# Where the gated activations of five down projections start in SBUF, relative to their weights, modulo 256 bytes

## The chip, the cores and the metric

The kernel runs on one core of a Trainium2 chip. The metric is device time in microseconds from launch to end. A core has TensorE (PE in the profile; PEld is its weight load, a row of its own that runs beside the matmuls), VectorE (DVE), ScalarE (ACT), GpSimd (POOL) and the DMA queues, here mostly that of SyncE (SP). Operands lie in SBUF, 128 partitions with the same byte address in each; TensorE reads both operands of a matmul from there and writes to PSUM. Below, the *distance* of a matmul is the address of its stationary operand minus the address of its moving operand, modulo 256 bytes.

## The reference, cut to what matters

A stack of two blocks works on 256 tokens of width 1024, all float32. It holds five feed-forward layers of this form (4 in the first block, 1 in the second, which has 16 more tokens in its mixer and the same 256 in its feed-forward layer), with a gated delta-rule mixer, a windowed attention and a retention and latent attention mixer between them:

```python
def swiglu(h, w_gu, w_down):
    gate, up = jnp.split(h @ w_gu, 2, axis=-1)
    return (jax.nn.silu(gate) * up) @ w_down

x = x + 0.5 * swiglu(rmsnorm(x, ffn1_norm[layer]), ffn1_w_gu[layer], ffn1_w_down[layer])
```

The inner width is 2816, so a down projection is a product of 256 x 2816 by 2816 x 1024.

## The kernel before, in words

Activations lie transposed, width on the partitions: `X[d]` is a 128 x 256 tile of the residual stream. A float32 product is made of three matmuls in the type `fp32r`: each operand is split into a high part and the remainder, and `lin` (lines 365 to 375) adds high x high, high x low and low x high for every 128-row piece of the contraction. The weight is the stationary operand (128 columns), the activation the moving one (256 columns). `Stream` loads weights in chunks of 128 x 2048 from SP's queue and splits each piece of 512 columns into `whi` (ScalarE, line 355) and `wlo` (VectorE, line 356), eight buffers each, from which TensorE takes slices of 128 columns.

`ffn` (line 459 on) runs five times, named "10", "20", "11", "21" and "30" in the order of the program. It first makes 44 gate and up projections of 24 matmuls each from `xh` and `xl`, the split and normed input. For each of 22 pairs it forms `ffg` and `ffu`, multiplies them, and splits the result into `ah` and `al`. The down projection then makes 8 output tiles, each of 22 x 3 = 66 matmuls with `ah` or `al` moving and `whi` or `wlo` stationary, and adds each to `X[d]`. `after(d)` prepares the next stage's input. Nothing is scheduled elsewhere: the order on each engine is that of the code.

Addresses follow from the order in which pools are opened. A `Home` has a pool `lines`, for tiles of whole multiples of 512 bytes, and a pool `rest`. Fill tiles that nothing reads or writes (`fill_cp`, `fill_sp`, `fill_wp`) move what is opened after them; the last is 512 - `LEAD` bytes long, and `LEAD` is 64. In the built program every `whi` and `wlo` slice starts at 32 modulo 256, and every `xh`, `xl`, `ah`, `al`, `dec`, `oh`, `ol` that `lin` moves past them starts at 224. The distance is thus 64 in the products that `lin` makes with 128 weight columns. A product with fewer columns goes through distances: in that of the delta rule's gates (`Stream("aba")`, 16 weight columns) one slice starts 64 bytes after the other, and the distance is 64, 128, 192 and 0 in turn, changing with every triple. The few other `fp32r` products lie outside `lin` or turn the roles round: the retention's scores (lines 1108 to 1110, distance 0, 64 contraction rows, 256 columns) and two small projections of the latent attention (line 1272 is one: the weight moves with 384 columns and the activation is stationary; distance 192).

Of the kernel before, what the change touches and what calls it, by code (L numbers as in the profile page):

```python
# [9 lines left out]
F32 = mybir.dt.float32  # L10
# [7 lines left out]
P = 128  # L18
# [13 lines left out]
LEAD = 64  # L32
CP_FILL = 320
SP_FILL = 448

# [184 lines left out]
def kernel(ctx: ExitStack, tc: tile.TileContext, dram: dict, out: bass.AP, dump=None):  # L222
# [8 lines left out]
    @contextmanager  # L231
    def home(name):
        with tc.tile_pool(name=name, bufs=1) as lines, tc.tile_pool(name=name + "r", bufs=1) as rest:
            yield Home(lines, rest)

    def pool(name, bufs=1, **kw):
        return ctx.enter_context(tc.tile_pool(name=name, bufs=bufs, **kw))
# [4 lines left out]
    rest = pool("sp", 2)  # L242
    rest.tile([P, SP_FILL // 4], F32, tag="fill", name="fill_sp", bufs=1)
    sp = Home(None, rest)
# [7 lines left out]
    def nm(base):  # L252
        uid[0] += 1
        return f"{base}_{uid[0]}"

    def sb(at, shape, tag, dt=F32, bufs=None):

        kw = {} if bufs is None else {"bufs": bufs}
        free = int(np.prod(shape[1:]))
        whole = -(-free * 4 // LINE) * LINE // 4  # L260
        if not isinstance(at, Home):
            return at.tile(shape, dt, tag=tag, name=nm(tag), **kw)
        if at.lines is None or whole != free and (dt != F32R or free * 4 < LINE):
            return at.rest.tile(shape, dt, tag=tag, name=nm(tag), **kw)
        if whole == free:
            return at.lines.tile(shape, dt, tag=tag, name=nm(tag), **kw)
        assert len(shape) == 2
        return at.lines.tile([shape[0], whole], dt, tag=tag, name=nm(tag), **kw)[:, :free]

    def bank(pool, shape):  # L270
        return pool.tile(shape, F32, tag="bank", name=nm("bank"))
# [95 lines left out]
    def lin(o, st, off, xs, w=P, n=S, ks=None):  # L367

        last = len(xs) - 1
        for k in range(len(xs)) if ks is None else ks:  # L370
            xh, xl = xs[k]
            wh, wl = st.at(off + k * w, w)
            mm(o, wh, xh[:, :n], start=k == 0, stop=False)  # L373
            mm(o, wl, xh[:, :n], start=False, stop=False)  # L374
            mm(o, wh, xl[:, :n], start=False, stop=k == last)  # L375

    def split(src, hi, lo):
        A.copy(hi, src)  # L378
        V.tensor_tensor(lo, src, f32(hi), op=ALU.subtract)  # L379
# [60 lines left out]
    def opening(norm, jobs, stats=None, n=S, at=(5, 1)):  # L440


        a, b, c = ((lambda ks, j=j: lin(*j[0], ks=ks, **j[1])) for j in jobs)
        stats = stats or (lambda: rnorm_nat(norm.ssq, D))
        a(range(KD - 1))
        b(range(at[0]))
        if at[0] < KD - 1:
            rn = stats()
        b(range(at[0], KD - 1))
        a([KD - 1])  # L450
        b([KD - 1])
        if at[0] >= KD - 1:
            rn = stats()
        c(range(at[1]))
        r = row_bcast(rn, n)
        c(range(at[1], KD))
        return r

    def ffn(name, norm, after, scale, hook=None, gu=None, first=None):

        with home(nm("ffn")) as fp:
            gu = gu or Stream("gu" + name)
            acts = []
            def proj(i):
                return bank(ps, [P, S]), gu, i * D, norm.xs

            pre = {i: proj(i) for i in range(3)}
            if first:
                first()
            r = opening(norm, [(pre[i], {}) for i in range(3)], at=(KD - 1, 3) if first else (5, 1))  # L470
            for m in range(KF):
                for i in (2 * m, 2 * m + 1):
                    if i not in pre:
                        pre[i] = proj(i)
                        lin(*pre[i])
                pg, pu = pre.pop(2 * m)[0], pre.pop(2 * m + 1)[0]
                g = sb(fp, [P, S], "ffg", bufs=2)
                V.tensor_tensor(g, pg, r[:, :S], op=ALU.mult)  # L478
                u = sb(fp, [P, S], "ffu", bufs=2)
                V.tensor_tensor(u, pu, r[:, :S], op=ALU.mult)  # L480
                A.activation(g, g, AF.Silu)  # L481
                V.tensor_tensor(u, g, u, op=ALU.mult)  # L482
                ah = sb(fp, [P, S], f"ah{m}", F32R)
                al = sb(fp, [P, S], f"al{m}", F32R)
                split(u, ah, al)
                acts.append((ah, al))
            dn = Stream("dn" + name)
            for d in range(KD):
                pd = bank(ps, [P, S])
                lin(pd, dn, d * FF, acts)  # L490
                if hook:
                    hook(d, pd)
                V.scalar_tensor_tensor(X[d][:, :S], pd, scale, X[d][:, :S], op0=ALU.mult, op1=ALU.add)
                after(d)
# [929 lines left out]
    def squares():  # L1424
# [6 lines left out]
        load_rest()  # L1431

    ffn("10", n, feed("mix_norm0"), 0.5, None, gu, squares)
    if dump:
        dump("x1", X[0][:, :S])
    n = cur[0]
    deltanet(n, feed("ffn2_norm0"))
    if dump:
        dump("x2", X[0][:, :S])
    n = cur[0]  # L1440
    ffn("20", n, feed("ffn1_norm1"), 0.5)
    n = cur[0]
    ffn("11", n, feed("mix_norm1"), 0.5)
    n = cur[0]
    window(n, feed("ffn2_norm1"))
# [94 lines left out]
```

## Time and profile before

| | us |
|---|---|
| median of 3 runs | 1472.96 (1472.29 to 1474.13) |
| the profiled execution, its own time | 1473.83 |
| its span, first to last instruction | 1472.0 |
| PE busy in it | 1443.5 (98%) |
| PEld busy | 1405.1 (95%) |
| DVE / ACT / POOL busy | 1107.7 / 858.2 / 114.1 |

[...] What a run of matmuls costs is the difference of the starts, called the *cadence* below: three rows of `lin` make a triple. A share of busy time near 100% says that the engine had work, not that it streamed a column in every cycle. [...]

### The profile page before, as it was taken

How to read it: one execution, taken by the hardware profiler on the slowest of the kernel's cores; microseconds unless marked ns; L12 is line 12 of the kernel's file. 1: busy time of each engine (PE TensorE's matmuls, PEld its weight loads, DVE VectorE, ACT ScalarE, POOL GpSimd, SP SyncE). 2: the span in 40 equal slices, each digit the busy share in tenths (PEclk: the TensorE clock that was granted, in tenths of full speed). 3: DMA queues.
4: the chain of work that ended last, by engine and by line, in shares of the span. 5: the costliest groups of instructions: out<-in, count | busy, mean ns of one | idle time of the engine just before them, and what ended most of it. 6: DMA issues, size and time to landing. Idle time of an engine off the chain costs nothing.

```text
span 1472.0 us, 31018 instructions
## 1 busy us (share of the span) xinstructions
PE 1443.5 (98%) x12318; PEld 1405.1 (95%) x12318; DVE 1107.7 (75%) x2340; ACT 858.2 (58%) x1767; POOL 114.1 (8%) x123
## 2 busy tenths in 40 slices
PE   8999999998999999999999999999999999999997
PEld 8999999988999999999997999999999889999997
DVE  6877668886877767777678877788877758777764
ACT  6655567655655555555547655665545756665552
POOL 2000141101100010000100100012001000100000
PEclk9999999999999999999999999999999999999998
DMA  7655443551555555555550555555432425555551
GB/s 254 224 195 201 171 148 116 166 167 33 181 191 198 201 189 185 201 195 187 193 199 30 201 178 195 177 196 172 134 113 91 144 87 195 207 199 187 193 197 58
DMA packets 46368, 248.34 MB, mean 169 GB/s; under 512 B 11408, under 2 KB 16272, under 8 KB 17168
## 3 DMA queue, kind: packets, MB, share of 16 engines
q1 hardware_dynamic: 45680, 245.87, 49.0%
q8 instruction: 97, 1.59, 0.4%
q10 hardware_dynamic: 544, 0.50, 0.1%
q14 instruction: 47, 0.39, 0.1%
HBM read 243.99 MB, written 2.36 MB: 167 GB/s over the span
## 4 chain that ended last, share of the span: by engine, by line
PE 86%; DVE 7%; ACT 2%; DMA 2%; issue 1%; POOL 1%; DVEq 0%; POOLq 0%; ACTq 0%; SPq 0%
PE bank L375 26%; PE bank L373 26%; PE bank L374 26%; DVE wlo L356 2%; PE bank L1130 1%; PE bank L1350 1%; DVE cv L652 1%; ACT whi L355 1%; PE bank L979 1%; DMA tc<-s 1%; PE bank L1319 1%; DVE xl L395 0%; DMA s<-tb 0%; PE bank L969 0%; POOL rr L383 0%
## 5 line engine op out<-in xcount | busy, mean ns | idle before, releaser
L356 DVE TENSOR_TENSOR wlo<-raw,whi 128x512 fp32r<-128x512 f32 x922 | 641.2, 700 | 257.4 <-ACT whi L355 255.9
L355 ACT CAST whi<-raw 128x512 fp32r<-128x512 f32 x922 | 565.4, 618 | 444.8 <-PE bank L375 407.3
L373 PE MATMUL bank<-xh,whi 128*128 128x256 f32 (+1 forms) x2488 | 697.0, 280 | 1.3 <-DVE xt L513 1.0
L374 PE MATMUL bank<-xh,wlo 128*128 128x256 f32 (+1 forms) x2488 | 692.9, 279 | 2.1 <-DVE wlo L356 2.1
L375 PE MATMUL bank<-xl,whi 128*128 128x256 f32 (+1 forms) x2488 | 692.3, 278 | 1.1 <-DVE xl L395 1.0
L374 PEld LDWEIGHTS bank<-xh,wlo 128*128 128x128 f32 x2488 | 468.5, 188 | 3.6 <-DVE wlo L356 3.1
L373 PEld LDWEIGHTS bank<-xh,whi 128*128 128x128 f32 x2488 | 466.9, 188 | 4.2 <-issue 2.1
L375 PEld LDWEIGHTS bank<-xl,whi 128*128 128x128 f32 x2488 | 466.9, 188 | 2.2 <-DVE xl L395 1.7
L375 PE MATMUL bank<-al,whi 128*128 128x256 f32 x880 | 243.8, 277 | 0.0
L373 PE MATMUL bank<-ah,whi 128*128 128x256 f32 x880 | 243.8, 277 | 0.0
L374 PE MATMUL bank<-ah,wlo 128*128 128x256 f32 x880 | 243.8, 277 | 0.0
L374 PEld LDWEIGHTS bank<-ah,wlo 128*128 128x128 f32 x880 | 165.9, 189 | 0.0
L375 PEld LDWEIGHTS bank<-al,whi 128*128 128x128 f32 x880 | 165.2, 188 | 0.0
L373 PEld LDWEIGHTS bank<-ah,whi 128*128 128x128 f32 x880 | 165.2, 188 | 0.0
L407 POOL TENSOR_TENSOR ssq<-sq,ssq 128x256 f32<-128x256 f32 (+1 forms) x72 | 63.8, 886 | 1080.4 <-ACT sq L406 1070.8
L378 ACT CAST ah<-ffu 128x256 fp32r<-128x256 f32 x110 | 44.7, 407 | 26.2 <-DVE ffu L482 26.1
L482 DVE TENSOR_TENSOR ffu<-ffg,ffu 128x256 f32<-128x256 f32 x110 | 46.7, 425 | 4.6 <-ACT ffg L481 1.2
L478 DVE TENSOR_TENSOR ffg<-bank,r 128x256 f32<-128x256 f32 x110 | 46.6, 424 | 2.8 <-PE bank L375 2.2
L481 ACT ACTIVATE ffg<-ffg 128x256 f32<-128x256 f32 x110 | 45.3, 414 | 5.7 <-DVE ffg L478 5.4
L480 DVE TENSOR_TENSOR ffu<-bank,r 128x256 f32<-128x256 f32 x110 | 46.6, 423 | 0.3
L379 DVE TENSOR_TENSOR al<-ffu,ah 128x256 fp32r<-128x256 f32 x110 | 46.0, 418 | 0.5 <-ACT ah L378 0.5
L373 PE MATMUL bank<-dec,whi 128*128 128x256 f32 x128 | 36.7, 286 | 0.0
(360 smaller groups left out, 1426.4 us busy)
## 6 DMA issues: line engine op xcount, KB each, us to landing
raw<-gu SPq DMA_DIRECT2D x109, 1024.0 KB, 4.8
raw<-dn SPq DMA_DIRECT2D x55, 1024.0 KB, 4.9
raw<-wret SPq DMA_DIRECT2D x12, 1024.0 KB, 4.9
raw<-aqk SPq DMA_DIRECT2D x8, 1024.0 KB, 4.8
raw<-wga SPq DMA_DIRECT2D x8, 1024.0 KB, 4.8
raw<-bin SPq DMA_DIRECT2D x6, 1024.0 KB, 4.9
raw<-az SPq DMA_DIRECT2D x4, 1024.0 KB, 4.8
raw<-av SPq DMA_DIRECT2D x4, 1024.0 KB, 4.9
```

The source lines that it names most:

```text
L355: A.copy(hi[:, :n], raw[:, o : o + n])
L356: V.tensor_tensor(lo[:, :n], raw[:, o : o + n], f32(hi[:, :n]), op=ALU.subtract)
L373: mm(o, wh, xh[:, :n], start=k == 0, stop=False)
L374: mm(o, wl, xh[:, :n], start=False, stop=False)
L375: mm(o, wh, xl[:, :n], start=False, stop=k == last)
L378: A.copy(hi, src)
L379: V.tensor_tensor(lo, src, f32(hi), op=ALU.subtract)
L407: G.tensor_tensor(acc[:, :n], q[:, :n], acc[:, :n], op=ALU.add)
L478: V.tensor_tensor(g, pg, r[:, :S], op=ALU.mult)
L480: V.tensor_tensor(u, pu, r[:, :S], op=ALU.mult)
L481: A.activation(g, g, AF.Silu)
L482: V.tensor_tensor(u, g, u, op=ALU.mult)
```

## The change

Each `ffn` opens its pool `lines` with a fill tile whose length depends on the layer. Nothing reads or writes it. It moves `ah`, `al`, `ffg` and `ffu` of that layer up by so many bytes; their pool is closed at the end of the layer, so no other tile moves.

```diff
+PLACE = {"10": 128, "20": 32, "11": 224, "21": 160, "30": 96}
...
     def ffn(name, norm, after, scale, hook=None, gu=None, first=None):

         with home(nm("ffn")) as fp:
+            if PLACE[name]:
+                fp.lines.tile([P, PLACE[name] // 4], F32, tag="fill", name=nm("fill_fp"))
             gu = gu or Stream("gu" + name)
             acts = []
```

In the built program the activations of the five down projections start at 96, 0, 192, 128 and 64 modulo 256, in the order "10", "20", "11", "21", "30", where all started at 224; the weights stay at 32. The distances are 192, 32, 96, 160 and 224. Every engine has the same instructions in the same order with the same waits.

## Rows read from the trace of the kernel before

**Rows 1.** The page: busy time by engine; the chain that ended last, by engine and line.

```profile
PE 1443.5 (98%) x12318; PEld 1405.1 (95%) x12318; DVE 1107.7 (75%) x2340; ACT 858.2 (58%) x1767; POOL 114.1 (8%) x123
...
PE 86%; DVE 7%; ACT 2%; DMA 2%; issue 1%; POOL 1%; DVEq 0%; POOLq 0%; ACTq 0%; SPq 0%
PE bank L375 26%; PE bank L373 26%; PE bank L374 26%; DVE wlo L356 2%; PE bank L1130 1%; PE bank L1350 1%; DVE cv L652 1%; ACT whi L355 1%; PE bank L979 1%; DMA tc<-s 1%; PE bank L1319 1%; DVE xl L395 0%; DMA s<-tb 0%; PE bank L969 0%; POOL rr L383 0%
```

**Rows 2.** The page's costliest groups: matmuls of the down projections; last number: idle before.

```profile
L373 PE MATMUL bank<-ah,whi 128*128 128x256 f32 x880 | 243.8, 277 | 0.0
```

**Rows 3.** Tile `ah` in each down projection: ns min/median/max, first and last start.

```profile
L373 PE MATMUL bank<-ah,whi x176: 276/276/276, 135.2 to 194.7; 128*128 128x256 f32 x176
...
L373 PE MATMUL bank<-ah,whi x176: 276/276/276, 503.9 to 563.4; 128*128 128x256 f32 x176
...
L373 PE MATMUL bank<-ah,whi x176: 276/276/276, 684.4 to 743.9; 128*128 128x256 f32 x176
...
L373 PE MATMUL bank<-ah,whi x176: 281/281/281, 953.0 to 1014.9; 128*128 128x256 f32 x176
...
L373 PE MATMUL bank<-ah,whi x176: 276/276/276, 1400.8 to 1460.3; 128*128 128x256 f32 x176
```

**Rows 4.** Windows of "10" down, "11" gate/up, "21" gate/up, "21" down; columns first.

```profile
core 0: us, PE busy (x) PEld busy (x) DVE busy (x) ACT busy (x) POOL busy (x), PEclk, DMA share, GB/s
...
135.00:195.00 60.00, 60.00 (x532) 60.00 (x531) 37.67 (x62) 32.43 (x59) 5.23 (x6) 1.00 0.54 188
...
570.00:684.00 114.00, 114.00 (x1008) 114.00 (x1007) 89.06 (x171) 67.81 (x128) 0.00 (x0) 1.00 0.57 192
...
834.00:952.00 118.00, 118.00 (x1005) 118.00 (x1004) 90.31 (x172) 68.98 (x132) 0.00 (x0) 1.00 0.55 187
952.00:1015.00 63.00, 63.00 (x538) 63.00 (x537) 53.24 (x99) 42.45 (x81) 12.44 (x12) 1.00 0.54 183
```

**Rows 5.** Timeline of PE after a pause, in "21" and "30": start, duration.

```profile
834.22 0.60 PE L435 MATMUL bank<-tabs,rn 128*128 128x128 f32 x4
834.58 0.36 PE L373 MATMUL bank<-xh,whi 128*128 128x256 f32 x1
834.78 0.28 PE L374 MATMUL bank<-xh,wlo 128*128 128x256 f32 x1
834.90 0.28 PE L375 MATMUL bank<-xl,whi 128*128 128x256 f32 x1
835.02 0.28 PE L373 MATMUL bank<-xh,whi 128*128 128x256 f32 x1
...
1286.96 0.29 PE L374 MATMUL bank<-xh,wlo 128*128 128x256 f32 x1
1287.08 0.28 PE L375 MATMUL bank<-xl,whi 128*128 128x256 f32 x1
1287.20 0.28 PE L373 MATMUL bank<-xh,whi 128*128 128x256 f32 x1
...
1287.43 0.28 PE L375 MATMUL bank<-xl,whi 128*128 128x256 f32 x1
1287.54 0.28 PE L373 MATMUL bank<-xh,whi 128*128 128x256 f32 x1
```

**Rows 6.** Timeline of PE: the delta rule's gates, 16 weight columns, four distances in turn.

```profile
195.07 0.28 PE L373 MATMUL bank<-xh,whi 128*16 128x256 f32 x1
...
195.41 0.28 PE L373 MATMUL bank<-xh,whi 128*16 128x256 f32 x1
...
195.75 0.28 PE L373 MATMUL bank<-xh,whi 128*16 128x256 f32 x1
...
196.09 0.28 PE L373 MATMUL bank<-xh,whi 128*16 128x256 f32 x1
...
197.11 0.28 PE L373 MATMUL bank<-xh,whi 128*16 128x256 f32 x1
```

**Rows 7.** Timeline of PE: the retention's scores, distance 0.

```profile
1038.54 0.28 PE L1108 MATMUL bank<-rk1h,rk0h 64*128 64x256 f32 x1
1038.66 0.28 PE L1109 MATMUL bank<-rk1l,rk0h 64*128 64x256 f32 x1
1038.78 0.28 PE L1110 MATMUL bank<-rk1h,rk0l 64*128 64x256 f32 x1
```

**Rows 8.** Timeline of PE: a latent projection with moving weights, 384 columns, distance 192.

```profile
1147.08 0.34 PE L1273 MATMUL bank<-whi,cl 128*128 128x384 f32 x1
1147.25 0.34 PE L1274 MATMUL bank<-wlo,ch 128*128 128x384 f32 x1
...
1148.12 0.34 PE L1273 MATMUL bank<-whi,cl 128*128 128x384 f32 x1
```

## The prediction, written before the result was known

> **What bounds the kernel now.** The page comes first: TensorE has work for 98% of the span and holds 86% of the chain that ended last, nearly all of it on the three lines of `lin` [rows 1]. So only the time of a matmul, or a pause between matmuls, counts. The down projections, 2640 matmuls in three groups of 880, had no idle time before them [rows 2]; the windows of one show VectorE busy for 37.67 of 60 us, ScalarE for 32.43, and DMA at 0.54 [rows 4]. None of these is near becoming the bound, so whatever a matmul of a down projection gains or loses goes straight to the end of the kernel.
>
> Next the cadence. In tile `ah`, first and last start are 175 triples apart. In "10" that is 194.7 - 135.2 = 59.5 us, 0.340 us a triple, 0.1133 us a matmul; "20", "11" and "30" agree to the tenth of a microsecond. In "21" it is 1014.9 - 953.0 = 61.9 us, 0.1179 us a matmul [rows 3]. The gate and up projections ahead show the same pair: about 1008 matmuls take 114 us in "11" and 1005 take 118 us in "21" [rows 4]. [...] So the kernel has **two cadences for one and the same distance**, a fast one of 0.1133 us and a slow one of 0.1179 us, and a stretch keeps the one it falls into. After a pause both first show 0.12 us; in "21" it stays near that, in "30" it drops to 0.11 after four or five matmuls [rows 5]. [...]
>
> **The change part by part.** No instruction is added, removed or moved, and no wait changes; the fill tile costs no instruction. `ffg`, `ffu`, `ah` and `al` move by 32 to 224 bytes. Should VectorE or ScalarE write them more slowly, the slack just named hides it (VectorE 89.06 and ScalarE 67.81 of 114 us during gate and up projections, rows 4); cost nothing, and if this cover went, the last `ah` of a layer would arrive late, five times. What is left is the cadence in 5 x 528 matmuls. One nanosecond in all of them is 2.64 us.
>
> What a new distance does to the cadence no row shows for this shape, so I bound it.
>
> From above: the retention's scores at distance 0 start 0.12 us apart [rows 7]. [...] For the four fast layers 4 x 528 x 0.0067 = 14.1 us, for "21" 528 x 0.0021 = 1.1 us: **+15 us**.
>
> From below: four matmuls of 128 columns with full weight loads take 0.60 us against 0.28 us for one, so (0.60 - 0.28)/3 = 0.107 us apart [rows 5]. [...] Allowing 0.110 us, half way to the fast cadence, the gain would be 4 x 528 x 0.0033 = 7.0 us and 528 x 0.0079 = 4.2 us in "21": **-11 us**.
>
> Between them: with 16 weight columns the distance passes through 64, 128, 192 and 0, and the starts stay 0.34 us apart per triple, first to last (197.11 - 195.07)/6 [rows 6]. That says that the distance at the start of a load does not set the cadence; but the load is an eighth as long there, so it does not say that a full load keeps out of the moving operand's way. I take the two cadences of rows 3 as the only ones held over hundreds of matmuls of this shape; the 0.12 us of rows 7 is three matmuls long and looks like the start-up of rows 5. A layer whose distance changes has to find its cadence anew at its first down matmul, and nothing in the rows favours the fast one. So of the four fast layers I let two fall to the slow cadence, each 528 x 0.0046 = 2.4 us, together 4.9 us, and leave "21" where it is. From the profiled execution's 1473.83 us (a span of 1472.0 and 1.8 around it) that makes 1478.7 us; from the median, 0.9 us lower, 1477.8 us. I name **1478 us**.
>
> The work between the layers keeps its addresses, and its cadence is settled after a pause [rows 5], so I charge nothing there. If a later stretch did fall to the other cadence, its price would be some 1000 x 0.0046 = 4.6 us, either way.
>
> The row says that cadence differs while both operands stay where they are. [...]
>
> **The rivals.**
>
> *The distance has no part in it.* For it: rows 6, and the two cadences at one distance [rows 3]. [...] All five layers keep their cadence, "21" perhaps falling into the fast one for 2.4 us less: 1471 to 1474 us, call it 1473 us.
>
> [...]
>
> [...]
>
> *Every other distance is worse.* The weight load, 128 columns long, meets the moving operand in the same part of SBUF, and distance 64 is the one that avoids it: the bound from above, 0.12 us everywhere, +15 us: 1488 us.
>
> *The change does nothing.* A fill that is never used might have been dropped; the built program has the new addresses, so this is out.
>
> **How the numbers follow.** Forecast (one to four layers fall to the slow cadence, +2 to +10 us) 0.34; no part 0.27; faster start 0.21; all worse 0.18. The range from 1463 to 1490 us takes in all four centres with a few microseconds on the outside of the last two; by itself the forecast has 1475 to 1483 us. A difference of 0.2%, 2.9 us, is about the least that a measurement of this kernel can tell from none. Slower: 0.18 and most of 0.34 (all but one layer's worth), 0.47. Same: 0.27 and the rest, less a little for a faster "21", 0.31. Faster: 0.22.
>
> **What would show it.** First and last start of `ah` in each layer give five cadences. Forecast: each is 0.113 or 0.118 us, with at least one change among the four. No part: 0.1133 four times. [...] All worse: 0.12 and above. Gate and up projections should keep 114 us, 118 us in "21"; if they change, the step that the work between keeps its cadence is wrong. A distance with a cadence far beyond 0.12 us, or pauses inside a down projection, would upset the bounds.

## The result: 1.0% slower, and where it was lost

The changed kernel took 1488.57 us (median of 4, 1482.55 to 1490.64) against 1472.62 us; the ratio is 1.0102, 95% interval 1.007 to 1.0134. Timed once more in a later session it was 1.0086, 1.0053 to 1.012 (e11 below). The range of the prediction, 1463 to 1490 us, holds it, and the likelier sign was right; but the forecast of 1478 us had a third of the loss, and the time lies outside the forecast's own 1475 to 1483 us.

The profiled execution took 1487.61 us, with a span of 1485.8 us, 13.8 us more than before. The page's engines and columns of tile `ah` in the five layers (ns min/median/max, first and last start), to be held against [rows 1, 3]:

```profile
PE 1455.4 (98%) x12318; PEld 1416.9 (95%) x12318; DVE 1107.9 (75%) x2340; ACT 858.5 (58%) x1767; POOL 113.7 (8%) x123
```

```profile
L375 PE MATMUL bank<-ah,whi x176: 279/279/282, 140.2 to 202.0; 128*128 128x256 f32 x176
...
L375 PE MATMUL bank<-ah,whi x176: 277/280/285, 514.7 to 576.9; 128*128 128x256 f32 x176
...
L375 PE MATMUL bank<-ah,whi x176: 277/280/282, 697.9 to 759.5; 128*128 128x256 f32 x176
...
L375 PE MATMUL bank<-ah,whi x176: 277/279/283, 964.3 to 1027.3; 128*128 128x256 f32 x176
...
L375 PE MATMUL bank<-ah,whi x176: 277/279/281, 1413.2 to 1474.5; 128*128 128x256 f32 x176
```

PE's busy time grew by 11.9 us with the same 12318 matmuls; VectorE and ScalarE did not move. The five rows span 61.8, 62.2, 61.6, 63.0 and 61.3 us where they spanned 59.5, 59.5, 59.5, 61.9 and 59.5 [rows 3]: 309.9 against 299.9, so **10.0 us of the 13.8 are in the down projections**, and all five grew. The cadences (span over 525 matmuls, here and below from starts to 0.01 us, since the rows are rounded to 0.1) are 0.1178, 0.1183, 0.1173, 0.1200 and 0.1167 us. Three of them stand in no row of before.

The other 3.8 us are the gaps between the rows, first start less the last start of the layer ahead. Up to layer "10" the gap is 140.2 against 135.2 us (+5.0); from "10" to "20" 312.7 against 309.2 (+3.5); from "20" to "11" 121.0 both times; from "11" to "21" 204.8 against 209.1 (-4.3); from "21" to "30" 385.9 both times; behind the last 11.3 against 11.7 (-0.4). No instruction in these gaps changed, and no address apart from those of `ffg`, `ffu`, `ah` and `al`, which are written there. What did change shows in windows inside the gate and up projections of "10" and "21" of the changed kernel (busy time and instructions by engine, clock, DMA), and of "10" before:

```profile
core 0: us, PE busy (x) PEld busy (x) DVE busy (x) ACT busy (x) POOL busy (x), PEclk, DMA share, GB/s
40.00:135.00 95.00, 95.00 (x809) 95.00 (x808) 72.91 (x137) 54.08 (x102) 0.00 (x0) 1.00 0.58 199
...
850.00:960.00 110.00, 110.00 (x973) 110.00 (x972) 86.18 (x166) 66.19 (x125) 0.00 (x0) 1.00 0.57 194
```

```profile
40.00:134.00 94.00, 94.00 (x832) 94.00 (x831) 73.86 (x141) 55.83 (x105) 0.00 (x0) 1.00 0.59 202
```

809 matmuls in 95 us are 0.1174 us each, 973 in 110 us are 0.1131, and 832 in 94 us before are 0.1130. So "10" ran its gate and up projections at the slow cadence and "21" at the fast one; before it was the other way round [rows 4 for "21"]. The granted clock, a share of its full speed, is 1.00 in all three windows.

The +3.5 us between "10" and "20" have another source. In that gap, which holds the delta rule mixer, the granted clock of the changed kernel's execution stood at 0.50 in three stretches; before, it did so in one (columns as above, the clock third from the end):

```profile
220.80:224.20 3.40, 3.40 (x18) 3.40 (x18) 2.31 (x4) 2.32 (x5) 1.25 (x1) 0.50 0.02 7
282.30:285.70 3.40, 3.40 (x18) 3.40 (x18) 2.01 (x13) 0.94 (x2) 2.13 (x1) 0.50 0.65 270
316.40:323.20 6.80, 6.80 (x64) 6.27 (x63) 3.59 (x14) 1.36 (x4) 0.00 (x0) 0.50 0.36 113
```

```profile
333.30:336.70 3.40, 3.40 (x19) 3.40 (x18) 3.40 (x5) 0.59 (x1) 1.56 (x1) 0.50 0.00 0
```

By the starts of the same matmuls in both traces, the three stretches took 5.8 us longer than before, and the one 1.6 us less after the change: 4.2 us together, which covers the +3.5. In some 20 us ahead of each fall TensorE had work for 86 to 95% of the time, at a clock of 1.00. No address in the mixer changed, and the 14 traces have between 3.4 and 17.1 us at the lower clock there, so this is not put to the change.

### The profile page after: what moved, and what is told of

The parts are those of the page before. It is cut to its first block, busy times and chain, and to the rows that moved or that the text cites. A ratio compares the mean times of both kernels' runs of the same rounds, so it can differ in the third digit from the quotient of the medians.

```text
span 1485.8 us, 31018 instructions
## 1 busy us (share of the span) xinstructions
PE 1455.4 (98%) x12318; PEld 1416.9 (95%) x12318; DVE 1107.9 (75%) x2340; ACT 858.5 (58%) x1767; POOL 113.7 (8%) x123
## 4 chain that ended last, share of the span: by engine, by line
PE 88%; DVE 6%; ACT 2%; issue 1%; DMA 1%; POOL 1%; SPq 0%; DVEq 0%; POOLq 0%; ACTq 0%
PE bank L375 26%; PE bank L377 26%; PE bank L376 26%; DVE wlo L358 2%; PE bank L1134 1%; PE bank L1354 1%; ACT whi L357 1%; PE bank L983 1%; DVE cv L656 1%; PE bank L1323 1%; DVE xl L397 0%; PE bank L711 0%; PE bank L973 0%; DMA xt<-xt 0%; DVE pe L946 0%
## 5 line engine op out<-in xcount | busy, mean ns | idle before, releaser
L377 PE MATMUL bank<-al,whi 128*128 128x256 f32 x880 | 246.8, 280 | 0.0
```

## Experiments

Theory A: the distance sets which cadences a stretch can have. Against it stood B, that the layer or its moment decides, and C, that the start of the moving operand alone does. Each experiment is one edit of the kernel before or of the changed one. All cadences below are first to last start of tile `ah` over 525.

### e1: the same places in other layers

```diff
-PLACE = {"10": 128, "20": 32, "11": 224, "21": 160, "30": 96}
+PLACE = {"10": 96, "20": 128, "11": 64, "21": 192, "30": 32}
```

> The five layers 10, 20, 11, 21, 30 get the distances 224, 192, 0, 128 and 32 instead of 192, 32, 96, 160 and 224. Theory A (the distance sets the cadence: a distance that is an odd multiple of 32 lacks the fast cadence of 0.1133 us, a multiple of 64 has it and the slow one of 0.1178): layer 10 at 0.1167 and layer 30 at 0.1183, as layers 30 and 20 had them at these distances; 20, 11 and 21 at 0.1133 or, where the gate and up projections ahead run slow, 0.1178. Theory B (the layer or its moment decides, the distance has no part): 10 at 0.1178, 20 at 0.1183, 11 at 0.1173, 21 at 0.1200, 30 at 0.1167 as in the changed kernel. Time by A about 1477 us, by B 1485 us.

Measured, tile `ah` in the five layers in order:

```profile
L375 PE MATMUL bank<-ah,whi x176: 277/279/281, 138.5 to 199.8; 128*128 128x256 f32 x176
...
L375 PE MATMUL bank<-ah,whi x176: 279/279/282, 514.9 to 576.8; 128*128 128x256 f32 x176
...
L375 PE MATMUL bank<-ah,whi x176: 280/283/283, 697.9 to 760.9; 128*128 128x256 f32 x176
...
L375 PE MATMUL bank<-ah,whi x176: 279/281/285, 965.8 to 1028.1; 128*128 128x256 f32 x176
...
L375 PE MATMUL bank<-ah,whi x176: 277/280/285, 1413.9 to 1476.0; 128*128 128x256 f32 x176
```

Layer "10" at distance 224 spans 61.3 us, as "30" did there in the changed kernel; "30" at 32 spans 62.1, as "20" did (62.2); "20" at 192 spans 61.9, as "10" did (61.8). At each of the three distances the cadence went with the distance into another layer: B falls. But A was too kind to multiples of 64: distance 0 has 63.0 us (0.1200) and 128 has 62.3 us (0.1187), both behind fast gate and up projections. The time, 1489.52 us, was a miss for A's 1477.

### e2 and e8: every address moved, every distance kept

```diff
-CP_FILL = 320
+CP_FILL = 352
```

> The kernel before with every tile 32 bytes further up: all distances stay, but activations start at 0 and weights at 64 modulo 256, both on a multiple of 64. Theory A (the distance decides): down projections at 0.1133 or 0.1178 us, time within 0.3% of the kernel before. Theory C (the start of the moving operand modulo 64 decides): the cadences of the layers 20, 11, 21 and 30 of the changed kernel, 0.1167 to 0.1200 us, in all products, some 30 us slower.

Activations now start at 0 and weights at 64 modulo 256. "10" and "21", the other three the same:

```profile
L373 PE MATMUL bank<-ah,whi x176: 276/276/276, 133.9 to 193.4; 128*128 128x256 f32 x176
...
L373 PE MATMUL bank<-ah,whi x176: 276/276/276, 949.2 to 1008.7; 128*128 128x256 f32 x176
```

59.5 us in all five, 0.1133. C falls, and with it the "faster start" of the prediction's chances: with the activations at 0 the cadence is the one they had at 224. The execution took 1467.46 us, 7 us less than the kernel before beside it; e8 asks whether that is a gain.

> The kernel with every tile 32 bytes further up and all distances kept, timed. If its 1467.5 us came from layer 21 falling into the fast cadence by chance, the ratio to the kernel before is 0.998 to 1.002. If the addresses themselves favour the fast cadence after a pause, it is 0.994 to 0.997.

The ratio to the kernel before is 0.9998, 0.9965 to 1.003. In the trace of these runs "10" had the slow cadence throughout, which no layer had in e2. A gain of 7 us (a ratio of 0.995) is outside the interval: the single execution of e2 was a lucky one, with all five stages fast.

### e3: the weights moved instead

```diff
-LEAD = 64
+LEAD = 96
-SP_FILL = 448
+SP_FILL = 480
```

> The kernel before with the weights 32 bytes further up and all activations where they were (224): distance 96 in all products of lin with 128 weight columns, gate and up projections included. Theory A (the distance decides): 0.1173 us as layer 11 of the changed kernel had at this distance, in down, gate and up projections alike; about 8500 of the matmuls, most of them from 0.1133, so 20 to 35 us slower. Theory C (the start of the moving operand decides): it stays at 224, so 0.1133 or 0.1178 and no change of time beyond 5 us.

1508.67 us, 34 us slower. Tile `ah` in "10" and "20", and a window in the gate and up projections of "20":

```profile
L373 PE MATMUL bank<-ah,whi x176: 277/280/282, 138.1 to 199.7; 128*128 128x256 f32 x176
...
L373 PE MATMUL bank<-ah,whi x176: 277/281/283, 516.6 to 578.9; 128*128 128x256 f32 x176
```

```profile
402.00:514.00 112.00, 112.00 (x946) 112.00 (x945) 84.77 (x159) 62.84 (x118) 0.00 (x0) 1.00 0.54 183
```

No activation moved, and "10", "11" and "30" span 61.6 us, exactly what "11" had in the changed kernel with its activation moved to the same distance of 96. "20" and "21" span 62.3 us (0.1187), so 96 has two cadences of its own. The gate and up projections follow (112 us / 946 = 0.1184). It is the pair of addresses that counts. At 224, where the activations also were before, "10" has 0.1173 us here and 0.1133 there: these rows show that a matmul's cadence depends on where the two operands lie relative to each other, and not on the start of the moving operand alone.

### e4 and e9: a shorter weight load at the same places

```diff
-                lin(pd, dn, d * FF, acts)
+                lin(pd[:16], dn, d * FF, acts, m=16)
...
+            if m:
+                wh, wl = wh[:, :m], wl[:, :m]
```

> The changed kernel with 16 instead of 128 weight columns in the down projections (112 of 128 rows of each output tile are left out): same starts, same distances, same moving operand, a weight load an eighth as long. If weight load and moving operand get in each other's way along the load (theory A1), the five cadences return to 0.1133 us at all distances. If it is where the two start relative to each other, or the moving operand alone (theory A2), they stay at 0.1167 to 0.1200 in layers 20, 11, 21 and 30.

```profile
L377 PE MATMUL bank<-ah,whi x176: 276/276/279, 138.5 to 198.0; 128*16 128x256 f32 x176
...
L377 PE MATMUL bank<-ah,whi x176: 276/276/279, 508.6 to 568.1; 128*16 128x256 f32 x176
...
L377 PE MATMUL bank<-ah,whi x176: 277/279/279, 689.3 to 750.5; 128*16 128x256 f32 x176
...
L377 PE MATMUL bank<-ah,whi x176: 277/279/280, 959.7 to 1021.0; 128*16 128x256 f32 x176
...
L377 PE MATMUL bank<-ah,whi x176: 277/279/283, 1406.8 to 1468.0; 128*16 128x256 f32 x176
```

At distances 192 and 32 the spans fall to 59.5 us, the fast cadence; at 96, 160 and 224 to 61.2 to 61.3 us, 0.1167, which at 224 is no fall at all. So the weight load's length is part of the price in four of five places, and neither A1 nor A2 holds as written. It fits [rows 6], which the prediction read with a warning: with a load of 16 columns the distances 0, 64, 128 and 192 look alike there, and e4 confirms 192.

> The changed kernel with 64 instead of 128 weight columns in the down projections (half of each output tile's rows are left out). With 16 columns distances 192 and 32 had 0.1134 us and 160, 96 and 224 had 0.1167. If the weight load's columns cost in proportion to how many there are beside the moving operand (theory A1), cadences lie between those of 16 and of 128 columns: 32 between 0.1134 and 0.1183, 160 between 0.1167 and 0.1200. If it is where single reads of the two meet, the distance 160 or 32 may be at either end already with 64 columns.

With 64 columns, distances 32 and 96:

```profile
L377 PE MATMUL bank<-ah,whi x176: 277/279/280, 514.5 to 575.8; 128*64 128x256 f32 x176
...
L377 PE MATMUL bank<-ah,whi x176: 279/283/283, 696.8 to 759.8; 128*64 128x256 f32 x176
```

32 lies between (61.3 us, 0.1167), and so do 192 (61.3) and 160 (62.1 us, 0.1183); but 96 takes 63.0 us (0.1200), more than with the full load (61.6), and 224 takes 61.8 against 61.3. A price in proportion to the load falls. Whether and how the reads of the two meet is left open.

### e5: 192 everywhere

```diff
+PLACE = {"10": 128, "20": 128, "11": 128, "21": 128, "30": 128}
```

> All five down projections at distance 192. In the two layers seen so far at 192 the gate and up projections ahead ran at the slow cadence and the down projection at 0.1178. Theory A3 (192 is as good as 64: it keeps the cadence with which it is entered): layers entered from 0.1133 run at 0.1133, those entered from 0.1178 at 0.1178; time as the kernel before, ratio 0.997 to 1.004. Theory A4 (64 alone has the fast cadence): 0.1178 in all five, 4 to 5 x 2.35 us, 9 to 12 us slower, ratio 1.006 to 1.008.

Windows in the gate and up projections of "20" and "21", then `ah` in the same two layers:

```profile
400.00:510.00 110.00, 110.00 (x973) 110.00 (x972) 86.18 (x165) 65.38 (x123) 0.00 (x0) 1.00 0.57 193
850.00:960.00 110.00, 110.00 (x937) 110.00 (x936) 83.65 (x158) 63.96 (x120) 0.00 (x0) 1.00 0.56 188
```

```profile
L375 PE MATMUL bank<-ah,whi x176: 279/279/279, 512.5 to 574.4; 128*128 128x256 f32 x176
...
L375 PE MATMUL bank<-ah,whi x176: 279/279/282, 966.4 to 1028.3; 128*128 128x256 f32 x176
```

"20" is entered at the fast cadence (973 in 110 us), "21" at the slow one (937); both run at 0.1178, as do the other three. A3 falls, A4 holds: 192 has the slow cadence alone. Ratio 1.0069, 1.0035 to 1.0102, that is 10 us; five layers at 2.35 us would be 12 us, less where the kernel before has a slow layer itself.

### e6: steps of 4 to 16 bytes around 64

```diff
-                ah = sb(fp, [P, S], f"ah{m}", F32R)
+                ah = sb(fp, [P, S + 32], f"ah{m}", F32R)[:, OFF[name] : OFF[name] + S]
```

(`al` likewise.)

> Distances 48, 56, 72, 80 and 60 in the layers 10, 20, 11, 21 and 30, by slicing the activations out of wider tiles. Theory A (the fast cadence belongs to a stretch of distances around 64, at least 16 bytes wide to each side): 0.1133 us in all that are entered fast. If it belongs to 64 alone, or to multiples of 16 or 32: 0.115 to 0.120 in 56, 72 and 60. If some place is better than 64: under 0.113.

```profile
L376 PE MATMUL bank<-ah,whi x176: 278/282/288, 133.6 to 196.1; 128*128 128x256 f32 x176
...
L376 PE MATMUL bank<-ah,whi x176: 282/283/285, 507.9 to 570.9; 128*128 128x256 f32 x176
...
L376 PE MATMUL bank<-ah,whi x176: 282/282/286, 692.1 to 755.1; 128*128 128x256 f32 x176
...
L376 PE MATMUL bank<-ah,whi x176: 280/281/282, 959.9 to 1022.5; 128*128 128x256 f32 x176
...
L376 PE MATMUL bank<-ah,whi x176: 280/282/285, 1407.8 to 1470.8; 128*128 128x256 f32 x176
```

62.5 to 63.0 us, 0.1192 to 0.1200, in all five; even 4 bytes from 64 cost 3.5 us a layer. A's "stretch around 64" falls. Nothing better than 64 was found. One rival is left: these are also the only starts off a multiple of 32 (240, 232, 216, 208 and 228 modulo 256), and whether part of the 3.5 us belongs to such a start, and not to the distance, was not separated.

### e7: the kernel before once more

> The kernel before once more, nothing changed but a comment. If the cadence of a stretch of distance 64 is drawn anew in each execution, the layer 21 (slow in the first trace) or another changes its cadence and down projections follow their gate and up projections. If it is fixed by the program, layer 21 runs at 0.1178 again and all others at 0.1133.

1486.9 us. `ah` in "20" and "11":

```profile
L373 PE MATMUL bank<-ah,whi x176: 281/281/281, 514.6 to 576.4; 128*128 128x256 f32 x176
...
L373 PE MATMUL bank<-ah,whi x176: 276/276/276, 697.6 to 757.1; 128*128 128x256 f32 x176
```

"20", fast in [rows 3], is slow here, and its gate and up projections with it (936 matmuls in 110 us); "21" is slow again. So the program does not fix the cadence of a stretch at distance 64; it differs between executions (so it does between e2 and e8, and between the two traces of the changed kernel). Over 13 traces (all but e3) 15 of 65 gate and up stages were slow: "10" and "21" six times each, "20" three times, "11" and "30" never. All 28 down projections at distance 64 in these traces had the cadence of the stage ahead. "10" was slow in five of the seven traces whose kernel moves its activations and in one of the six others; these are too few to tell whether the change has a part in that.

The traces also show where a stage gets its cadence. Some 50 matmuls into it stand four matmuls of another product, `rn` (line 435, 128 moving columns; the first line of [rows 5]). Ahead of them, in "21" and then in "30" of the first trace, three matmuls apart:

```profile
833.76 0.28 PE L375 MATMUL bank<-xl,whi 128*128 128x256 f32 x1
...
834.10 0.28 PE L375 MATMUL bank<-xl,whi 128*128 128x256 f32 x1
...
1285.92 0.28 PE L375 MATMUL bank<-xl,whi 128*128 128x256 f32 x1
...
1286.28 0.28 PE L375 MATMUL bank<-xl,whi 128*128 128x256 f32 x1
1286.39 0.61 PE L435 MATMUL bank<-tabs,rn 128*128 128x128 f32 x4
```

"21" arrives at the fast cadence (0.34 us for three) and leaves at the slow one, "30" arrives at the slow one (0.36 us) and leaves at the fast one. In the four layers behind "10", the matmuls just ahead of `rn` and the thousand behind it had opposite cadences in 51 of the 52 stages of these traces: 43 went from slow to fast, 8 from fast to slow, and one stayed slow. "11" and "30" arrived slow every time, and so ran fast in all 13 traces.

### e10: a nudge out of the slow cadence

```diff
+                if (name, m) in (("10", 6), ("20", 1), ("21", 1)):
+                    t = bank(pm, [P, 512])
+                    wh = gu.at((2 * m + 1) * D + 7 * P, 16)[0]
+                    for _ in range(6):
+                        mm(t[:16, :S], wh, norm.xs[0][0][:, :S], start=True, stop=True)
```

The idea came from the timeline of PE in e8, where the slow down projection of "10" runs into 16-column loads (start, duration):

```profile
200.42 0.28 PE L375 MATMUL bank<-al,whi 128*128 128x256 f32 x1
200.54 0.28 PE L373 MATMUL bank<-xh,whi 128*16 128x256 f32 x1
200.66 0.28 PE L374 MATMUL bank<-xh,wlo 128*16 128x256 f32 x1
...
201.00 0.28 PE L374 MATMUL bank<-xh,wlo 128*16 128x256 f32 x1
201.11 0.28 PE L375 MATMUL bank<-xl,whi 128*16 128x256 f32 x1
201.23 0.28 PE L373 MATMUL bank<-xh,whi 128*16 128x256 f32 x1
```

Starts 0.12 us apart become 0.11 to 0.12 apart.

> The kernel before with six matmuls of 16 weight columns put into the gate and up projections of layers 10, 20 and 21, the layers that were at times slow: in the trace of e8 a stretch at distance 64 left the slow cadence within three matmuls when such short loads came, and stayed fast with full loads after them. Cost 18 x 0.1133 = 2.0 us. If short loads end the slow cadence: gate, up and down projections of all five layers at 0.1133, some 5 to 8 us gained on average, ratio 0.994 to 0.998 with the cost. If the cadence is drawn anew each time: as often slow as before, ratio 1.000 to 1.003.

The ratio is 1.0003, 0.9979 to 1.0027: no gain. In the traced execution all three stages were fast before the nudge reached them ("20" and "21" had gone from slow to fast at `rn`, just ahead of it), so it does not show whether six short loads end a slow stretch. Inconclusive; no kernel here beats the one before.

### e11 and e12: the changed kernel again, and 256 bytes further

> The changed kernel once more, timed beside the kernel before in the same session. If its down projections are bound to their distances: the same five cadences as in its first trace, 0.1178, 0.1183, 0.1173, 0.1200 and 0.1167 us, whatever the gate and up projections do, and a ratio of 1.004 to 1.010: 10 us less what the kernel before loses where its own down projections run slow.

Spans of `ah` 61.8, 62.1, 61.6, 63.0 and 61.3 us: the same five cadences, this time with all five gate and up stages fast. At 192, 32 and 224, which were entered from slow and from fast stages (e1, e5, e12), the cadence is the same either way; 0, 128 and 160 were entered from fast stages alone, and 96 has a second value in e3. Ratio 1.0086, 1.0053 to 1.012.

> Activations moved by 256 bytes and more: the distances modulo 256 are 192, 64, 64, 32 and 64 in the layers 10, 20, 11, 21 and 30, but modulo 512 each is 256 away from where it was measured so far. If the distance counts modulo 256: 0.1178 in 10, 0.1133 in 20, 11 and 30 (0.1178 in one whose gate and up projections run slow), 0.1183 in 21. If it counts modulo 512 or more: other cadences, in 20, 11 and 30 above all.

"20", "11" and "21":

```profile
L375 PE MATMUL bank<-ah,whi x176: 281/281/281, 510.3 to 572.1; 128*128 128x256 f32 x176
...
L375 PE MATMUL bank<-ah,whi x176: 276/276/276, 693.3 to 752.8; 128*128 128x256 f32 x176
...
L375 PE MATMUL bank<-ah,whi x176: 277/281/285, 962.3 to 1024.4; 128*128 128x256 f32 x176
```

"11" and "30" have the fast cadence, "21" at 32 has 62.1 us as in e1, and "20" is slow behind slow gate and up projections (936 in 110 us). Modulo 256 is the right period, as far as a step of 256 shows it.

### The places in one table

| distance | span of `ah`, us | cadence, us | seen in |
|---|---|---|---|
| 64 | 59.5, or 61.8 behind a slow stage | 0.1133 / 0.1178 | before, e2, e7, e8, e10, e12 |
| 0 | 63.0 | 0.1200 | e1 |
| 32 | 62.1 | 0.1183 | after, e1, e11, e12 |
| 96 | 61.6 or 62.3 | 0.1173 / 0.1187 | after, e3, e11 |
| 128 | 62.3 | 0.1187 | e1 |
| 160 | 63.0 | 0.1200 | after, e11 |
| 192 | 61.8 | 0.1178 | after, e1, e5, e11, e12 |
| 224 | 61.3 | 0.1167 | after, e1, e11 |
| 48, 80 | 62.6, 62.6 | 0.1192, 0.1193 | e6 |
| 56, 60, 72 | 63.0 | 0.1200 | e6 |

## Why the prediction was right, and where its steps failed

**The bound.** Right. Whatever a down matmul gained or lost went to the end: 10.0 us in the five rows, none of it hidden, and no engine beside PE moved.

**The two cadences.** Read rightly in the trace of before, and the slow one is what layer "10" has at distance 192. But the step "I take the two cadences of rows 3 as the only ones" failed: they belong to distance 64. Six of the seven other multiples of 32 have cadences of their own, 0.1167 to 0.1200 us, and the changed kernel had the same five in both its traces; only 96 showed a second value (e3).

**Two of the four fast layers fall, and "21" stays.** This is the term that failed: 4.9 us was forecast, 10.0 us measured. It had a layer draw one of two cadences; the runs show that each distance sets its own. All four lost, by 2.3, 2.7, 2.1 and 1.8 us, only one of them to the slow cadence of before, and "21", slow already, still lost 1.1 us. The sign came out as forecast for another reason than the one given, and the range holds the time by 1.4 us, because it was drawn wide enough for the rival that every other distance is worse. To that extent the hit is luck.

**The bounds.** The bound from above, +15 us, held: its 0.12 us is what the worst distances, such as 0 and 160, measure. So the row of the retention's scores, set aside as "three matmuls long", was the better guide: distance 0 does have 0.1200 us over 528 matmuls. The bound from below was never approached. No run shows its 0.110 us for 256 columns; of all distances tried none goes under 0.1133 us. It was the author's estimate that 256 columns could come so near to the 0.107 us read for 128 columns, and the lower end of the range and the 0.21 for a faster start needed such a cadence too. The row was read a little low: the four short `rn` matmuls start 0.11 us apart, not 0.107, since the last takes 0.27 us and not 0.28.

**The work between the layers, charged at nothing.** Failed for a single execution. The step took the cadence as settled after a pause [rows 5]; the stages between keep their addresses, but which cadence a stage settles into differs from execution to execution, as e7 shows for the unchanged kernel. In the profiled pair the gate and up projections gave +5.0 us in "10" and -4.3 us in "21", and the granted clock in the delta rule mixer +3.5 us. The price named for a stage that changes, 4.6 us, fits the 5.0 and the 4.3.

**The rivals.** "The distance has no part" is out by e1 and e3. "Faster start" is out by e2, with 0.1133 us at a start of 0 as at 224. "Every other distance is worse" is what happened, at two thirds of its price (10.0 of 15 us, with 0.12 us in one of five layers). Of its mechanism, e1, e2 and e3 show that the place of the two operands relative to each other counts, and e4 that the length of the weight load has a part (at 160, 0.1167 us with 16 columns against 0.1200 with 128). That the two meet in the same part of SBUF is not shown; no run tells how they disturb each other. It had a chance of 0.18 and deserved more: [rows 7], which showed starts 0.12 us apart at another distance, spoke for it, and was set aside as short and as a start-up. [Rows 8] has nothing to be held against, since no row shows 384 columns at distance 64.

## What to carry to other kernels

Where matmuls with short streams follow each other without a pause, the addresses of stationary and moving operand relative to each other are a parameter to measure: here one distance modulo 256 bytes, in its fast cadence of 0.1133 us, was 3 to 6% faster in each matmul than the twelve others tried, one only 4 bytes away. In its slow cadence, 0.1178 us, it was not the best: 224 had 0.1167 us behind a slow stage too (e1). Measure several places in one execution, one to a layer, and read each from first and last start in the trace; the kernel's time alone cannot separate them. When the only row for a new condition is short or of another shape, as [rows 7] is, do not set it aside for the rows of the right shape that lack the condition.

## What was not expected of the hardware

The cadence at distance 64 has two values, 0.1133 and 0.1178 us at the same granted clock of 1.00, and which one a stage of 1000 matmuls gets differs between executions of one and the same program: some 4.4 us for a stage and 2.3 us for the down projection behind it. The first three executions of the kernel before lay within 2 us; in a later session single ones went from 1465.89 to 1494.33 us. The one execution of it that was traced in that session (e7, 1486.9 us) had two slow stages and 17.1 us at the lower clock in the mixer; how much of the spread the two explain in the others is not shown. In the profiled pair 3.8 us of the 13.8 came from them, and no run shows that the change had a part in it.

Behind four short matmuls of another product the cadence was the other of the two in 51 of 52 stages. That is read from the traces alone; no run moved these matmuls, so it is not shown that they are the cause, and what decides the cadence with which a stage arrives there stays open.
